# A hand-held order of instructions made anew: a decoder layer's queue table, planned with a longer hold of VectorE beside a POOL transfer issue

## The chip, the cores and the metric

The kernel runs on one core of one Trainium2 chip, in one launch. The metric is device microseconds of that core for the whole layer, lower is better. The engines are named as in the profile: PE is TensorE (PEld its weight loads), DVE is VectorE, ACT is ScalarE, POOL is GpSimd, SP is SyncE, which here only issues DMA transfers.

## The reference

One post-norm decoder layer, batch 1, sequence S = 512, width D = 1024, float32. Two token mixers read one combined projection; their gated sum is projected and added to the residual, and a gated FFN with a short convolution follows.

```python
h = x @ w_in[l]
y_a = nsa_attention(...) @ w_nsa_out[l]
y_b = gated_deltanet(...) @ w_gdn_out[l]
gate_a, gate_b = jnp.split(merge_gate, 2, axis=-1)
mix = (jax.nn.sigmoid(gate_a) * y_a + jax.nn.sigmoid(gate_b) * y_b) @ w_o[l]
x = layer_norm(DEEPNORM_ALPHA * x + mix, ln1_g[l], ln1_b[l])
f = conv_ffn(x, ffn_w_up[l], ffn_conv_w[l], ffn_w_down[l])
x = layer_norm(DEEPNORM_ALPHA * x + f, ln2_g[l], ln2_b[l])
```

The first mixer is sparse attention: 8 heads of 64 in two key groups, with three branches (compressed blocks, top-k selected blocks, a window), each a softmax with a linear position bias and a gate of its own. The second is gated DeltaNet: 4 heads of 128, a causal convolution of four taps and SiLU on q, k and v, and a chunked form with a triangular inverse per chunk of 64. The FFN is (silu(gate) * val) @ w_down, 2816 wide, after a causal convolution of three taps.

## The kernel before, in words

**Products.** Every large product is done with float32 split into a high and a low part. `split_w` (line 460) loads a block of weights into `raw` on SP's queue (line 463), rounds it into `wh` (line 470 on ACT, 472 on another engine) and takes the rest into `wl` (line 474, on DVE or POOL). `product` (line 479) then issues three matmuls for each contraction tile: wh with the high part (484), wh with the low part (486), wl with the high part (487). `raw`, `wh` and `wl` have three buffers each.

**Stages, by the time of the profile.** Until about 26 us x is transposed and split. From there to about 340 us steps of the two mixers are interleaved as a list ORDER says: for DeltaNet the projections with convolution (`conv_silu`, 635 to 655), `gdn_mid` (714 to 744), the triangular part `gdn_tri` (746 to 777) and `gdn_inv` (778 to 828); for the attention `cmp_attn` (993 to 1015: a softmax on DVE and ACT whose last step on DVE, line 1013, scales `cs`, which PE then transposes through `trans4`, line 659), `scores` (1030 to 1060) and `flip` (1062 to 1078). In `scores`, lines 1050 to 1059 take the reciprocal of a softmax's sum; where ACT scales the scores, DVE first multiplies the reciprocal by the gate (1056) and ACT scales (1057), and where POOL does, it does both in one operation (1059). From about 340 to 425 us come the merge gates (`merge`, 1118, a tanh at 1121) and the mixers' output projections (products into `pm`, merged at 1199 and 1201). The output projection with the first layer norm follows to about 490 us, then the FFN up to about 712 and the FFN down to the end.

**Sums in DRAM.** POOL issues transfers that add blocks of weights in DRAM (`sums_o`, line 503, into `osum`; `sums`, line 513, into `wsum`). `osum` is first read by a `raw` load on SP at 393 us, `wsum` after 700 us.

**What sets the order.** The instructions are emitted in one order by the program, with priorities. The table QUEUES (lines 133 to 333) then gives, for each of PE, DVE, ACT (as "Activation"), POOL and SP, the order in which that engine's instructions are to stand: each number is the n-th instruction of that engine in the program's order, a range stands for its members. The function `queues` (line 337) chains each engine's instructions in that order by scheduling-only dependencies. The instructions, tiles, buffers, engines and waits on data do not depend on the table; an engine works through its own list in order. The table comes from a planner outside the kernel that simulates the engines with a price for each operation.

Some numbers that the text below uses. PE: 452 is the first transpose of `cs` in `cmp_attn(0)` (line 659); 384-387 are four transposes of `kq` (line 659); 479 and 515-522 are matmuls of 128x512; 1969 is the last matmul of a `pm` product, 1942-1945 are matmuls of a `gps` product, and 1970 is the first matmul of the next `gps` product. POOL: 18 and 46 are `at` (line 743) of two heads, 31 is `th` (652), 32 `vraw` (653), 14 `rn` (525), 40 and 67 `wl` (474), 43 `grh` (720), 37 a cast of `vm` (1068), 29 and 30 tap sums (643), 64-66 `sc` (1059), 105 and 107 osum transfers (503), 140 and 141 wsum transfers (513). SP: 24 is the small load of `w` (line 939), 29-33 are `raw` loads.

Of the kernel before, what the change touches and what calls it, by code (L numbers as in the profile page):

```python
# [70 lines left out]
def layout(a):  # L71
# [72 lines left out]
488-489 752 740 490 509 491 741-742 492 541-542 753 493-494 754 743 495 510 496 543 511 546 755 497 544-545 512 547
756-757 498-499 744 758 500 548 759-760 549-551 560-561 761 745 762-765 562 565-566 766 552 767 746 553 768 554 537
555 591-592 563-564 567 538 568-569 539-540 581-582 769 570 593-596 556 597 557 598 558 599-600 770-771 559 571 583
585-586 796-797 772 584 572 798 573-575 773 587 601-602 576 799 577 774 800 588-589 801-806 603 606 590 604 651 578
605 607 579-580 807-810 608 653 811 620-621 609-611 652 812-813 654 814 612 815-816 622 625-626 613 623-624 614-616
864-865 627-628 641 629-630 642 866-870 617-618 871 619 643 645 872 631 646 873 644 632-633 874 634 875 647 876-877
635-636 699-700 648 637 649-650 638-639 878 640 701 879 704 702 880 817 705 881 703 818 882-886 706 718-719 707-709  # L150
887 720-721 819 838-839 722 710 655 659-660 656-658 661-662 840 854-855 711-712 841 663-666 842-843 713-715 856
667-669 671-678 670 857-858 716-717 844-845 679-686 860-861 859 846 862 687-694 863 1053 847-848 695-698 747-750
936-940 1054 941 1055 775 1056 776 1057 849 777-778 850 942-944 779 945-948 780 949-951 781-782 1058 952-954 783-784
# [24 lines left out]
1623-1624 1604-1605 1572 1625-1626 1573 1627 1574-1576 1628-1629 1634 1630-1632 1577-1579 1635-1638 1658 1639-1647
1580 1659 1648 1606-1609 1581 1660 1649 1661 1633 1650-1651 1662 1652 1663 1653 1664-1668 1654-1655 1669 1656
1670-1672 1657 1673 1682 1674-1676 1683 1677-1678 1684-1685 1679 1686-1687 1680 1688-1690 1694 1691 1681 1692-1693  # L180
1706-1707 1695-1696 1708 1697 1709-1711 1718 1712 1719 1713 1720 1698 1714 1699 1715 1721-1722 1700 1716 1701 1723
1717 1724-1725 1702 1726-1728 1703-1705 1729-1735 1754 1736-1737 1742-1746 1755 1747 1738 1748-1750 1739 1751 1756
1752 1757-1758 1753 1759-1772 1778-1779 1740-1741 1773 1780 1774 1781-1782 1775-1776 1783-1786 1777 1787-1789 1802
1790-1791 1803-1804 1814 1805-1807 1815 1808 1792 1809-1810 1816-1818 1811 1819-1820 1812 1821-1822 1813 1823-1825
1793-1794 1826 1795-1796 1827-1831 1797-1799 1832-1834 1800-1801 1835-1840 1850 1841-1842 1851-1855 1843 1856-1858
1844 1859-1861 1845 1862 1846-1849 1874-1878 1863 1879 1864 1886-1887 1865-1866 1880 1888 1867 1889 1881-1883 1868
1884 1869 1890 1885 1870 1891-1892 1898 1893-1897 1899 1871-1873 1900-1911 1922 1912 1923 1913-1914 1924 1915-1916
1925-1926 1917 1927-1928 1918 1929 1919 1930-1932 1920 1933-1934 1921 1935-1936 1946-1947 1937 1948 1938 1949 1958
1939-1942 1950-1954 1959-1960 1955-1956 1961 1957 1962-1964 1943-1944 1965-1969 1945 1970-1981 1994 1982 1995-1998
1983 1999 1984-1985 2000-2002 1986 2003-2004 1987 2005-2008 1988 2018 1989-1990 2019-2020 1991 2021 2009-2011 1992  # L190
2022-2024 2012-2013 2030 2014-2017 1993 2031 2025-2028 2032 2029 2033-2034 2042 2035 2043-2044 2036-2037 2054-2055
# [1380 lines left out]
```

## Time and profile before

| | before |
|---|---|
| median of 3 runs | 832.31 us (831.04 to 835.99) |
| the profiled execution | 831.55 us |
| its span, first to last instruction | 829.8 us |
| mean granted TensorE clock | 0.992 |
| PE busy | 809.2 us, 98% of the span |
| DVE, ACT, POOL busy | 602.5, 409.2, 180.5 us |
| moved by DMA | 119.58 MB, mean 144 GB/s |

The profile is one execution, the median is over others; the profiled execution's own time exceeds its span by what lies around the instructions. Times in rows are microseconds from the start of the span. A timeline row reads: start, duration, engine, source line, operation, output<-inputs, shapes, count, and in brackets the idle time of the engine before it with what ended the wait. A window row reads: window, its length, then busy time (count) of PE, PEld, DVE, ACT and POOL, the granted clock, the DMA engines' busy share, GB/s. A DMA row on an engine's own line is the issue of the transfer, not its flight.

### The profile page before, as it was taken

How to read it: one execution, taken by the hardware profiler on the slowest of the kernel's cores; microseconds unless marked ns; L12 is line 12 of the kernel's file. 1: busy time of each engine (PE TensorE's matmuls, PEld its weight loads, DVE VectorE, ACT ScalarE, POOL GpSimd, SP SyncE). 2: the span in 40 equal slices, each digit the busy share in tenths (PEclk: the TensorE clock that was granted, in tenths of full speed). 3: DMA queues.
4: the chain of work that ended last, by engine and by line, in shares of the span. 5: the costliest groups of instructions: out<-in, count | busy, mean ns of one | idle time of the engine just before them, and what ended most of it. 6: DMA issues, size and time to landing. Idle time of an engine off the chain costs nothing.

```text
span 829.8 us, 11767 instructions
## 1 busy us (share of the span) xinstructions
PE 809.2 (98%) x4138; PEld 673.8 (81%) x4138; DVE 602.5 (73%) x1339; ACT 409.2 (49%) x912; POOL 180.5 (22%) x176
## 2 busy tenths in 40 slices
PE   9999899999999999999999999999999999999996
PEld 8778688778888888888788898888888888878784
DVE  5656779979868976647549965667577577687897
ACT  4453487765576764513335333435334344574641
POOL 0333805141266111152200111102112101100001
PEclk9999999999999999999999999999999999999999
DMA  8333615134284711334365476333938932466583
GB/s 279 102 92 101 252 32 133 44 96 108 49 219 111 233 51 52 120 108 128 115 241 177 152 147 211 125 102 102 215 103 249 229 102 80 150 199 182 190 257 124
DMA packets 43979, 119.58 MB, mean 144 GB/s; under 512 B 3472, under 2 KB 4624, under 8 KB 43664
## 3 DMA queue, kind: packets, MB, share of 16 engines
q1 hardware_dynamic: 32144, 87.37, 32.3%
q0 software_dynamic: 11776, 31.46, 16.3%
q8 instruction: 33, 0.54, 0.3%
q14 instruction: 26, 0.21, 0.1%
HBM read 116.72 MB, written 33.55 MB: 181 GB/s over the span
## 4 chain that ended last, share of the span: by engine, by line
PE 82%; DVE 9%; DMA 4%; ACT 2%; issue 2%; POOL 1%; ACTq 0%; DVEq 0%; POOLq 0%; SPq 0%
PE pu L484 10%; PE pu L486 10%; PE pu L487 10%; PE gps L484 8%; PE gps L486 8%; PE gps L487 8%; DMA raw<-wsum 3%; PE pw L1288 3%; PE px L1452 3%; PE pu L1288 2%; PE pz L1452 2%; PE pout L1089 2%; PE pu L1452 2%; PE aps L1075 2%; PE pm L484 2%
## 5 line engine op out<-in xcount | busy, mean ns | idle before, releaser
L474 DVE TENSOR_TENSOR wl<-raw,wh 128x512 fp32r<-128x512 f32 x146 | 102.7, 705 | 78.0 <-ACT wh L470 38.6
L470 ACT ACTIVATE wh<-raw 128x512 fp32r<-128x512 f32 x126 | 79.1, 629 | 133.7 <-PE pu L486 97.0
L486 PE MATMUL pu<-ml,wh 128*128 128x512 f32 (+1 forms) x384 | 131.5, 373 | 0.0
L484 PE MATMUL pu<-mh,wh 128*128 128x512 f32 (+1 forms) x384 | 130.8, 372 | 0.4 <-ACT mh L1267 0.4
L487 PE MATMUL pu<-mh,wl 128*128 128x512 f32 (+1 forms) x384 | 130.8, 373 | 0.0
L484 PE MATMUL gps<-xh,wh 128*128 128x512 f32 x320 | 125.7, 404 | 3.2 <-ACT mt L1121 2.1
L486 PE MATMUL gps<-xl,wh 128*128 128x512 f32 x320 | 126.1, 401 | 0.0
L487 PE MATMUL gps<-xh,wl 128*128 128x512 f32 x320 | 124.4, 400 | 0.0
L484 PEld LDWEIGHTS pu<-mh,wh 128*128 128x128 f32 x384 | 71.3, 188 | 13.4 <-ACT mh L1267 0.7
L487 PEld LDWEIGHTS pu<-mh,wl 128*128 128x128 f32 x384 | 71.4, 188 | 13.0 <-DVE wl L474 0.5
L486 PEld LDWEIGHTS pu<-ml,wh 128*128 128x128 f32 x384 | 71.4, 188 | 12.6
L1410 DVE SCALAR_TENSOR_TENSOR fa<-pu,fcw,fa 128x511 f32<-128x511 f32 (+1 forms) x88 | 64.6, 744 | 17.5 <-ACT fa L1407 16.9
L1416 POOL TENSOR_TENSOR fth<-fth,fa 128x512 f32<-128x512 f32 x22 | 30.4, 1387 | 212.6 <-DVE fth L1415 186.3
L484 PEld LDWEIGHTS gps<-xh,wh 128*128 128x128 f32 x320 | 60.4, 190 | 15.1 <-issue 2.5
L487 PEld LDWEIGHTS gps<-xh,wl 128*128 128x128 f32 x320 | 60.8, 190 | 10.9
L486 PEld LDWEIGHTS gps<-xl,wh 128*128 128x128 f32 x320 | 61.0, 191 | 10.2
L1387 ACT ACTIVATE wh<-raw 128x512 fp32r<-128x512 f32 x67 | 40.1, 626 | 41.0 <-DMA raw<-in_down 13.5
L1388 DVE TENSOR_TENSOR wl<-raw,wh 128x512 fp32r<-128x512 f32 x67 | 44.8, 694 | 17.9 <-ACT wh L1387 17.3
L474 POOL TENSOR_TENSOR wl<-raw,wh 128x512 fp32r<-128x512 f32 x30 | 40.1, 1339 | 13.4 <-ACT wh L470 7.9
L525 POOL TENSOR_TENSOR rs<-rs,minus_half 128x1 f32<-128x1 f32 x8 | 7.2, 901 | 161.4 <-DVE rs L1246 161.4
L1407 ACT ACTIVATE fa<-pu,fcw 128x512 f32<-128x512 f32 x44 | 29.7, 680 | 24.8 <-PE pu L487 22.0
L1048 ACT ACTIVATE sc<-sc,mn 128x384 f32<-128x384 f32 (+2 forms) x64 | 35.7, 560 | 10.5 <-DVE mn L1046 10.1
(365 smaller groups left out, 1719.8 us busy)
## 6 DMA issues: line engine op xcount, KB each, us to landing
raw<-in_up SPq DMA_DIRECT2D x44, 512.0 KB, 3.7
raw<-in_wT SPq DMA_DIRECT2D x40, 512.0 KB, 3.6
wsum<-in_down POOLq DMA_DIRECT2D x6, 2816.0 KB, 20.8
raw<-wsum SPq DMA_DIRECT2D x20, 512.0 KB, 3.9
raw<-in_down SPq DMA_DIRECT2D x15, 512.0 KB, 4.3
osum<-in_wo POOLq DMA_DIRECT2D x6, 1024.0 KB, 9.0
wsum<-wsum POOLq DMA_DIRECT2D x2, 2816.0 KB, 14.6
raw<-in_wm SPq DMA_DIRECT2D x8, 512.0 KB, 3.5
```

What stands on the lines that cost most here:

```text
L470: A.activation(wh, r, AF.Copy)
L474: eng.tensor_tensor(wl, r, wh.bitcast(F32), op=OP.subtract)
L484: i = PE.matmul(ps, wh[k], mh_(k), start=(k == 0), stop=False)
L486: PE.matmul(ps, wh[k], ml_(k), start=False, stop=False)
L487: PE.matmul(ps, wl[k], mh_(k), start=False, stop=(k == n - 1))
L1048: A.activation(s[:, i, :n], s[:, i, :n], AF.Exp, scale=-1.0, bias=mn[:, 0, i:i + 1], accum_out=mn[:, 1, i:i + 1])
L1288: PE.matmul(ps[t], a[x](j)[:, ts], w[y][:, j % 2, :], start=fresh and j == 0 and i == 0, stop=j == TT - 1 and i == 2, skip_group_check=True)
L1387: A.activation(hi, raw[:, i], AF.Copy)
L1388: V.tensor_tensor(lo, raw[:, i], hi.bitcast(F32), op=OP.subtract)
L1410: V.scalar_tensor_tensor(acc[:, n:], ps[:, :S - n], w[:, i:i + 1], acc[:, n:], op0=OP.mult, op1=OP.add)
L1416: G.tensor_tensor(th, th, g[1], op=OP.mult)
L1452: m = PE.matmul(ps, a[x][:, j, ts], w[y], start=first and i == 0, stop=last and i == 2, skip_group_check=True)
```

## The change

Only the table QUEUES is replaced; no instruction, tile, buffer, engine or priority changes. The planner's prices had one rule added: a VectorE operation with two operands in SBUF that meets a transfer issue of POOL waits for POOL's next operation too. The table was made anew under it. 2349 of PE's 3880 places hold another instruction than before, 773 of DVE's 1275, 421 of ACT's 799, 91 of POOL's 172 and 15 of SP's 185. The first differences lie at 12 to 44 us; behind about 600 us no engine's order differs. Most instructions move by a few places. The core of the diff, with the lines that the text below speaks of:

```diff
     "PE": ...
-324-327 464-466 328 332-339 329-330 467 331 468-471 513 472 340-347 473 514 474-475 348-355 476-477 515 356-359 452
-384-387 516 478 517 479 501-502 453-455 412-415 518 503 519-521 504 522-526 440-441 527 442-443 723-724 528-529
...
+348-355 476-478 356-359 384-387 479 515-522 452 501 412-414 502 415 453-454 523-524 503 525-527 440-443 455 723-724
...
-1939-1942 1950-1954 1959-1960 1955-1956 1961 1957 1962-1964 1943-1944 1965-1969 1945 1970-1981 1994 1982 1995-1998
...
+1954 1961-1963 1955-1956 1964 1938 1965-1966 1939 1967-1968 1940 1957 1941 1969 1942-1945 1970-1991 1994-1997 1992
...
-    "Pool": """2 1 0 8 10 9 12 11 3 13 4-7 15-17 19-22 27-28 140 14 33 25 23 34 29 18 39 30 37 31 105 32 40 43 36 44 24 62 35 38 41
-45 54 107 48 26 55 104 42 49 51 47 52 92 66 108 68 67 46 65 64 69 57 50 58 109 87 56 53 59 61 63 75 60 144 77 80 110
...
+    "Pool": """2 1 0 8 10 9 11-12 3 13 4-7 15-17 19-22 27-28 33 23 25 34 141 140 29 39 30 18 31-32 14 40 37 43 105 24 38 26 44 36 35
+54 41 45 55 48 42 62 49 51 47 52 107 64 66 65 67 46 68 57 69 58 50 53 56 59 61 104 63 108 75 60 76 109 80 92 88 77 81
...
-    "SP": """0-7 17 8-9 15 25 10 12 11 13-14 19 18 16 20-23 26-28 24 29-75 80 76 79 77-78 81-134 136-165 167 135 169 171 173-178
...
+    "SP": """0-7 17 8-9 15 25 10 12 11 13-14 19 18 16 20-23 26-33 24 34-75 81 80 82-83 77-78 76 84 79 85-134 136-165 167 135 169
```

More of the change, by code (lines that the diff above doesn't have):

```diff
@@ L144 @@
[L144 to L153, printed above, removed]
@@ new lines @@
+1319-1320 1288-1289 1405-1406 1265-1266 1280 1267 1408 1268 1407 1281-1282 1269 1409 1270 1321-1323 1271 1324 1229
+1325 1290 1272 1326-1327 1291 1328-1329 1230 1330 1410 1292 1422 1293 1423 1294 1231 1411-1412 1232 1424 1413
+1425-1426 1295-1298 1414 1299-1301 1427 1302-1304 1379 1428 1415 1380-1381 1429 1416 1430-1432 1417-1419 1305 1382
+1443 1420 1444 1331-1332 1421 1383 1306 1384-1386 1433 1445 1447-1448 1387 1434 1388 1435 1389-1392 1436-1437 1333
+1449 1446 1393 1453 1477 1454 1478 1394 1438 1450 1455-1456 1451 1439 1395 1458 1452 1440 1396-1397 1479 1459 1480
@@ new lines @@
+1441 1481 1442 1482 1334 1460-1462 1457 1463 1472-1473 1398 1483-1485 1399-1401 1486 1402 1487-1488 1474 1464
+1501-1502 1465-1466 1475-1476 1467 1582 1489 1583 1490 1335 1503 1468 1517-1518 1339-1341 1504 1342 1336-1338
+1505-1506 1491-1494 1343-1346 1519-1520 1469 1495 1521 1470 1347-1348 1522 1351-1358 1349 1471 1507-1508 1350
+1509-1511 1496-1499 1512-1513 1359-1366 1523-1524 1544 1500 1545 1584-1585 1546 1367-1374 1525 1514 1547-1550
+1610-1611 1515-1516 1586-1588 1375-1378 1551 1526 1612-1613 1527 1552-1554 1589 1614 1528 1615 1563-1564 1529-1530
@@ new lines @@
+1590 1616 1591-1592 1531-1532 1617-1618 1533 1555 1619 1593 1534 1594 1535 1556 1595 1620 1596 1536-1537 1597-1598
+1538 1565 1599 1621-1622 1539-1540 1566-1567 1557-1558 1568-1569 1559 1600-1602 1541-1542 1570 1560 1571 1561
+1623-1626 1543 1562 1603 1627 1604-1605 1572-1577 1628-1629 1634 1630 1635 1631 1636-1639 1632 1640-1641 1578
+1606-1609 1579 1642-1643 1658 1644 1633 1645-1646 1580-1581 1647 1659-1660 1648 1661-1662 1649 1663-1667 1650-1651
+1668-1670 1652-1654 1671 1682 1655 1672 1656-1657 1673-1675 1683-1685 1676-1680 1686-1687 1681 1694 1688-1692 1695
@@ new lines @@
+1693 1706-1707 1696 1708-1709 1718 1697-1698 1710-1711 1699-1700 1712-1714 1701 1715-1716 1702 1719-1721 1703-1705
+1730 1722-1724 1717 1742 1725-1728 1731-1732 1743-1747 1733-1734 1754 1729 1755 1735 1748-1753 1736-1737 1756-1763
+1738-1740 1764-1769 1741 1770-1772 1778 1773-1774 1779 1775 1780-1782 1776 1783-1786 1777 1787-1788 1802 1789 1803
+1790 1804-1806 1814-1817 1807-1809 1818 1810-1811 1791 1812 1819 1792 1813 1793 1820-1822 1794 1823 1826 1795 1827
+1796 1824-1825 1828 1797-1798 1829-1830 1799-1800 1831 1801 1832-1838 1850-1852 1839-1840 1853-1858 1841 1859-1860
@@ new lines @@
+2035 2014 2036-2038 2015-2016 2042 2017 2029 2039 2043 2040 2054 2041 2055 2044-2051 2056 2052 2057-2059 2053
+2069-2070 2060 2071 2061 2066 2062-2063 2075-2076 2067-2068 2064-2065 2077 2072-2073 2081 2074 2090 2114 2093 2078
+2091 2094-2095 2099 2082 2092 2083 2096 2115 2079 2097 2117 2087 2098 2100-2101 2080 2084 2105 2118 2102 2106 2085
+2116 2103-2104 2108 2086 2088 2120-2121 2119 2089 2109 2123 2122 2107 2124-2126 2141 2129 2127 2142 2130 2110-2113
+2131 2135 2128 2132 2138 2143 2139 2133-2134 2136-2137 2140 2147-2149 2144-2145 2162 2146 2150 2163 2151-2156
@@ new lines @@
+2159-2160 2164 2161 2157-2158 2168-2170 2174-2176 2180-2182 2165-2167 2186-2187 2171-2173 2177-2178 2188 2179
+2189-2191 2195 2192-2193 2183-2185 2194 2196-2198 2210 2199-2200 2204-2206 2201 2211-2212 2202-2203 2207-2209
+2218-2220 2213 2224-2226 2221 2214 2230 2222 2215 2231-2232 2223 2236 2242 2227 2216 2243-2244 2228-2229 2245 2237
+2233-2235 2239 2274 2240 2238 2217 2250 2241 2338 2251-2252 2275 2306-2307 2276 2308 2253 2309 2254 2339 2310-2311
+2277-2278 2340 2255 2279 2246-2247 2256 2248 2280 2249 2341-2342 2312 2343 2313 2257 2281 2258 2282 2314 2344-2345
@@ new lines @@
+2259 2346-2347 2315 2283 2260 2284-2286 2348 2287 2316 2288 2261 2317-2319 2289-2290 2262 2291-2293 2263 2320-2321
+2264-2265 2349-2351 2266 2298 2294 2299-2300 2295 2322 2352-2353 2267 2301 2268-2269 2296 2354 2270 2302 2323 2303
+2355-2357 2271 2324 2304 2325 2297 2326 2358 2327 2330-2333 2359 2272 2328 2360 2273 2361 2329 2305 2362 2386 2410
+2434 2363 2387 2411 2364 2388-2390 2334-2337 2391-2392 2365 2393 2366 2435 2394-2395 2412 2396-2397 2436 2398 2413
+2367 2414 2399-2401 2437 2368 2415 2402 2416-2417 2438-2440 2418 2403-2407 2369-2374 2408-2409 2375 2419-2420
@@ new lines @@
+2441-2442 2376 2421 2443 2422 2377 2423 2444-2445 2378-2381 2424-2425 2382 2426 2383 2446 2384 2427-2428 2385 2429
+2482 2447-2449 2430 2483-2489 2450-2451 2431 2458 2490 2459-2460 2452 2432 2453 2433 2454 2461 2491-2492 2455
+2462-2463 2493 2464 2494-2495 2465-2472 2496 2456-2457 2497-2499 2506-2512 2473 2513 2474 2514-2516 2500-2501 2517
+2475 2502 2476-2478 2518-2519 2503 2479-2481 2520-2524 2504-2505 2530-2535 2525-2527 2536-2545 2528 2554 2546 2529
+2547 2555 2548-2551 2556 2552 2557-2558 2553 2559-2568 2578 2569-2570 2579-2589 2571-2572 2590-2591 2602 2592 2573
@@ new lines @@
+2593 2603-2605 2574-2576 2606-2610 2594 2577 2611 2595 2612-2613 2596-2599 2626-2627 2614 2628 2615 2629-2631 2600
+2632 2616 2601 2617 2633-2636 2618-2621 2637-2638 2650 2622 2639 2623 2640-2642 2651 2643 2624-2625 2652-2653 2644
+2654-2656 2645-2646 2657-2661 2647 2662 2648 2663-2666 2674 2667 2675 2649 2668 2676 2669-2671 2677-2678 2672-2673
+2679-2684 2698-2699 2685 2700-2706 2686 2707-2709 2687 2710 2688-2690 2722 2711 2723-2724 2691-2692 2725-2726
+2712-2714 2727-2728 2693-2695 2729 2715 2696 2716 2730 2717 2697 2731-2734 2718 2735 2719 2736 2720 2746-2748
@@ new lines @@
+2737-2739 2749-2751 2740 2752-2753 2741 2754-2755 2721 2756 2742 2757-2758 2743 2759 2770-2771 2760-2761 2772 2762
+2773 2744 2774-2776 2763 2777 2745 2778-2780 2764-2766 2781 2767 2794 2782 2795 2768-2769 2783 2796-2799 2784-2788
+2800-2802 2789-2792 2803-2804 2793 2805-2806 2818 2807-2808 2819-2820 2809 2821 2810-2815 2822-2824 2816 2825 2817
+2826-2830 2842-2843 2831 2844 2832-2833 2845-2849 2834 2850-2852 2835 2853 2836 2854-2860 2866 2837 2867 2861 2868
+2838 2869 2862 2870 2839-2840 2871-2874 2863 2875 2864 2841 2876-2878 2865 2879-2881 2890-2891 2882 2892 2883
@@ new lines @@
+2893-2902 2884-2886 2903 2914-2915 2904 2916-2917 2887 2918-2920 2905 2921 2888 2906 2922-2925 2889 2907-2908 2926
+2909 2927 2910 2938 2928 2939-2941 2911 2942-2943 2912-2913 2944 2929 2945-2950 2930-2931 2951 2962 2932 2963 2952
+2964-2965 2953-2954 2933 2966 2955 2967-2968 2934 2969 2935 2970-2971 2936 2972 2956 2973 2957-2959 2937 2960 2986
+2974-2975 2987 2961 2976-2978 2988-2991 2979 2992-2993 2980 2994 2981 2995-2996 2982 2997-3002 2983 3003 3010
+2984-2985 3004 3011-3012 3005 3013 3006-3007 3014 3008 3015 3009 3016-3018 3034 3019-3022 3035-3042 3023 3043-3044
@@ new lines @@
+3024 3045 3025-3026 3046 3027 3058 3047 3028-3029 3059 3048 3060 3030 3049 3061 3050 3031 3062-3063 3051 3032-3033
+3052 3064 3053 3065-3069 3054 3070-3071 3055 3082 3056-3057 3083-3091 3072 3092-3093 3073-3076 3106 3077-3078
+3094-3095 3107 3096 3108 3079 3109 3080-3081 3110-3113 3097-3098 3114-3116 3099-3100 3117 3101 3118 3102 3130-3131
+3103-3104 3132-3133 3105 3134-3137 3119 3138-3140 3120 3141-3142 3121 3143 3122-3125 3154 3126 3155-3156 3144 3157
+3145 3127-3129 3158 3146 3159-3162 3147 3163-3169 3178 3170 3179 3171 3180 3148 3181 3172 3182-3186 3149-3152 3173
@@ new lines @@
+3153 3187-3188 3174 3189-3190 3175 3191 3176 3192 3177 3202 3193-3194 3203-3206 3195-3200 3207-3214 3201 3226
+3215-3218 3227 3219-3220 3228 3221 3229 3222 3230 3223-3225 3231-3236 3250 3237 3251-3252 3238-3239 3253-3254 3240
+3255-3261 3241 3262-3263 3242-3244 3264 3274 3245 3275-3276 3265 3246-3247 3277-3280 3248 3281 3266 3249 3267
+3282-3286 3268-3269 3287 3270 3298 3271 3288-3289 3299 3272 3300 3290-3291 3301 3292 3302-3303 3273 3304-3306
+3293-3294 3307 3295 3308 3296 3309-3312 3322 3297 3313-3314 3323 3315 3324-3330 3316-3317 3331-3332 3318 3333-3335
@@ new lines @@
+3319 3336 3320 3346 3337-3338 3347 3339-3342 3348-3349 3343-3344 3350-3352 3345 3353 3370 3354 3321 3355 3371
+3356-3361 3372 3362 3373-3379 3363 3380 3364-3365 3381 3366-3367 3394-3395 3382 3368 3396 3383 3397-3402 3384 3403
+3369 3404 3385-3387 3405 3388-3390 3406 3391 3407 3392 3408 3418-3419 3409 3420 3393 3421-3424 3427 3410 3428 3411
+3429 3425 3412 3426 3413 3430-3431 3433-3434 3414 3435 3432 3436-3437 3439 3438 3440-3441 3415-3416 3442 3445-3446
+3443-3444 3447 3451 3448 3417 3449 3452-3453 3450 3454-3464 3466 3487 3465 3467 3469-3471 3475 3468 3488 3484-3485
@@ new lines @@
+3617 3549 3618 3599-3600 3604 3609 3605 3622 3621 3625 3606 3623-3624 3610 3626-3628 3611 3631 3629 3632 3630 3633
+3637 3613 3634-3635 3638-3639 3636 3640 3643 3641 3612 3642 3646 3614 3647 3644-3645 3615 3649 3648 3652-3653
+3650-3651 3654 3658 3655-3657 3661 3659 3662-3663 3660 3664 3685 3667 3665 3668 3666 3686 3682 3669 3673 3670 3687
+3691 3683 3671 3674 3672 3675 3679 3684 3692 3676 3688 3680 3689 3681 3690 3693-3694 3677 3695 3697 3696 3700
+3698-3699 3678 3701 3703 3702 3706 3704 3707 3705 3708-3714 3718-3719 3715-3716 3720 3717 3724 3721 3725-3726
@@ new lines @@
+3722-3723 3730 3727 3731 3728 3732 3729 3751 3733-3734 3752 3735 3739-3740 3736 3741 3745 3748-3749 3737 3750 3754
+3738 3742 3753 3746 3755 3747 3757 3743 3758 3756 3759-3760 3744 3761 3763 3762 3764 3766 3765 3769-3771 3767-3768
+3772 3775 3773-3774 3778-3779 3776-3777 3780 3784 3781-3783 3785 3787 3786 3790-3792 3796-3798 3788-3789 3802-3803
+3793 3804-3806 3794 3807 3795 3799-3801 3808-3820 3847-3848 3821-3825 3849 3826 3850-3851 3827-3828 3852-3853 3829
+3854-3855 3830-3836 3856 3837 3857 3838-3842 3858 3843-3844 3859 3845-3846 3860-3879""",
+    "DVE": """0 27 104 1-4 6 5 7 9 8 10-11 13 12 14-18 58-60 19 64 61 20 65 23 21-22 90 66 62 31-32 67 63 33 72 34-38 73 39 102
@@ new lines @@
+1008 990 999 1011 991 1012 1020 982 1002 993 1003 1021 1009 1024 968 1010 994-995 971 1025 1031 1004 1032 1013 1022
+1014 992 1035 1023 981 1036 1015 1044 1017 1045 1026-1027 1018 1048 1033-1034 1019 1037 1049 1055 1038 1056 1028 1016
+1059 1046-1047 1039 1006 1005 1060 1068 1050 1057 1069 1051 1072 1052 1058 1073 1041 1079 1061 1053 1062 1042 1080
+1040 1083 1054 1043 1070-1071 1074 1084 1075 1063 1092 1029-1030 1093 1096 1085 1065-1066 1086 1081 1097 1082
+1103-1104 1107 1076 1087 1094-1095 1108 1089 1078 1116 1088 1090 1098 1117 1099 1105 1064 1077 1120 1100 1091 1106
@@ L334 @@
+147 138-139 142 150 143 145 153 148 146 149 151-152 154-155 157 156 160 159 158 161 163 162 165 164 166-171""",
+    "SP": """0-7 17 8-9 15 25 10 12 11 13-14 19 18 16 20-23 26-33 24 34-75 81 80 82-83 77-78 76 84 79 85-134 136-165 167 135 169
+171 173-178 168 179-180 172 182 166 170 181 183-184""",
 }
```

286 lines of the change are left out of this document (102 added, 184 removed).

## The prediction

> **What bounds the kernel now.** I read the page's totals first.
>
> ```profile
> span 829.8 us, 11767 instructions
> PE 809.2 (98%) x4138; PEld 673.8 (81%) x4138; DVE 602.5 (73%) x1339; ACT 409.2 (49%) x912; POOL 180.5 (22%) x176
> PE 82%; DVE 9%; DMA 4%; ACT 2%; issue 2%; POOL 1%; ACTq 0%; DVEq 0%; POOLq 0%; SPq 0%
> ```
>
> TensorE is busy for 98% of the span and holds 82% of the chain that ended last. The diff adds and removes no instruction, so a new order can only win the time in which PE stands still or runs at half clock. The windows by stage tell where that is. Their columns are window, length, busy time of PE, PEld, DVE, ACT and POOL with counts, granted clock, DMA share, GB/s.
>
> ```profile
> 80.00:180.00 100.00, 93.74 (x592) 77.46 (x593) 83.73 (x266) 67.93 (x200) 43.93 (x47) 0.97 0.38 117
> 180.00:340.00 160.00, 159.77 (x963) 135.69 (x963) 122.99 (x386) 102.74 (x285) 47.73 (x47) 1.00 0.44 112
> 340.00:420.00 80.00, 77.67 (x335) 63.49 (x334) 46.89 (x71) 21.56 (x41) 22.49 (x22) 0.98 0.38 119
> 600.00:822.00 222.00, 221.12 (x963) 179.54 (x961) 168.13 (x271) 106.40 (x177) 22.23 (x17) 1.00 0.56 167
> ```
>
> PE is idle for 6.26 us between 80 and 180 and 2.33 between 340 and 420. Of these only those two show a granted clock under 1.00. Behind 600 us PE hardly stops (0.88 of 222), and no place in the tables moves there: that part has nothing to give or to lose. Looking closer at the weak stages finds three stalls, each followed by a stretch at half clock.
>
> ```profile
> 99.72:102.69 2.97, 0.00 (x1) 0.01 (x1) 2.97 (x2) 0.38 (x1) 2.91 (x4) 1.00 0.99 360
> 102.94:106.36 3.42, 3.42 (x14) 3.03 (x13) 0.75 (x4) 1.48 (x6) 0.97 (x1) 0.50 0.30 115
> 168.20:169.35 1.15, 0.00 (x1) 0.01 (x1) 1.15 (x5) 0.46 (x2) 0.50 (x1) 1.00 1.03 417
> 171.21:174.62 3.41, 3.41 (x27) 2.33 (x25) 1.80 (x5) 1.41 (x5) 2.08 (x3) 0.50 0.16 28
> 404.03:406.09 2.06, 0.00 (x1) 0.03 (x1) 1.19 (x2) 0.74 (x2) 2.06 (x2) 1.00 0.00 0
> 406.73:410.14 3.41, 3.41 (x10) 2.62 (x9) 3.01 (x7) 1.79 (x4) 0.00 (x0) 0.50 0.48 157
> ```
>
> Call them A (2.97 us), B (1.15) and C (2.06). A stretch of 3.41 us at 0.50 does 1.70 us less work than one at 1.00, so the three cost 6.18 + 5.10 = 11.3 us at most. That is the purse.
>
> **The change part by part: stall A.** In the timeline rows (start, duration) the stall is made by VectorE and POOL together.
>
> ```profile
> 98.12 4.52 DVE L1013 TENSOR_TENSOR cs<-cs,csm 128x512 f32<-128x512 f32 x1
> 96.56 1.28 POOL L652 TENSOR_TENSOR th<-th,acc 128x512 f32<-128x512 f32 x1 [0.46 <-ACT th L648]
> 97.78 0.76 POOL L503 DMA_DIRECT2D osum<-in_wo  x1
> 98.50 1.35 POOL L653 TENSOR_TENSOR vraw<-th,acc 128x512 f32<-128x512 f32 x1
> 99.74 1.33 POOL L474 TENSOR_TENSOR wl<-raw,wh 128x512 fp32r<-128x512 f32 x1
> 100.96 1.11 POOL L720 TENSOR_TENSOR grh<-cst,gdh 128x512 fp32r<-128x512 f32 x1
> 102.69 0.33 PE L659 MATMUL aps<-ident,cs 128*128 128x128 f32 x1 [2.97 <-DVE tiny L578]
> L1013 DVE TENSOR_TENSOR cs<-cs,csm x2: 684/2600/4516, 98.1 to 216.3; 128x512 f32<-128x512 f32 x2
> ```
>
> L1013 takes 0.684 us the other time and 4.516 here. It starts inside the osum issue and ends only when grh does, after three POOL operations that read SBUF back to back. PE's transpose at L659 (452 in the table) needs its result. The rule behind the new table has this shape, but it prices the hold at the issue and one operation, to 99.85, where the row shows three.
>
> The new table does two things. PE's run "384-387 479 515-522" now stands before 452: four transposes and nine large matmuls. Their prices:
>
> ```profile
> 457.85 3.40 PE pw L1288 x15
> 199.15 0.77 PE dps L659 x7
> ```
>
> The first gives 0.227 us each, the second 0.11, so the cover is 9 x 0.227 + 4 x 0.11 = 2.5 us and PE comes to 452 at 99.72 + 2.5 = 102.2. On POOL the transfer (105) goes from before vraw (32) to behind grh (43), and at (18) and rn (14) come into the run: "18 31-32 14 40". If that run has a gap, L1013 ends near 98.12 + 0.68 and the stall is gone. If not, from th's start it lasts at, th, vraw, rn, wl = 1.28 + 1.28 + 1.35 + 1.28 + 1.33 (at and rn estimated as th), to 103.1; L1013 ends at 103.8 and the gap is 1.6. I take the middle, 0.8, since nothing shows which: 2.17 less. The half clock goes in one case and stays in the other, 0.85 on average. **A: -3.0, bounds -1.4 (gap 1.6, slow stretch stays) and -4.7.**
>
> [...]
>
> ```profile
> 139.38 0.68 DVE L655 SCALAR_TENSOR_TENSOR kq<-th,acc 128x512 f32<-128x512 f32 x1
> 139.35 0.75 POOL L503 DMA_DIRECT2D osum<-in_wo  x1
> ```
>
> A two-input operation of 0.68 us that lies wholly in an issue of 0.75 is not stretched. So the issue is not enough; the unbroken run behind it counts.
>
> **Stall B** is the same hold without an issue beside it.
>
> ```profile
> 166.25 2.54 DVE L1056 TENSOR_TENSOR mn<-mn,gsig 128x1 f32<-128x1 f32 x2
> 166.19 1.29 POOL L474 TENSOR_TENSOR wl<-raw,wh 128x512 fp32r<-128x512 f32 x1
> 167.42 1.28 POOL L743 TENSOR_TENSOR at<-at,cst 128x512 f32<-128x512 f32 x1
> 170.95 0.56 POOL L1059 TENSOR_SCALAR sc<-sc,mn,gsig 128x256 f32<-128x256 f32 x1 [2.25 <-DVE mn L1050]
> 169.35 0.33 PE L1075 MATMUL aps<-ident,sc 128*128 128x128 f32 x1 [1.15 <-ACT sc L1057]
> ```
>
> Two products of one column take 2.54 us, over wl and at. In the new table these (67 and 46) stand behind sc (64-66), which waits for a reciprocal after 168; so POOL waits while mn runs. A hold of over 2 us leaves, more than the 1.15 that PE lost; the gap goes. Of the 1.70 of half clock I count half, as smaller gaps just ahead stay (1.32 us at 164.18, quoted below) and 1.15 was enough for a slow stretch. What is behind sc now, wl first, comes up to 3 us later, and its product waits for it; PE has other products there. **B: -2.0, bounds -1.15 and -2.85.**
>
> **Stall C** is a chain through the merge.
>
> ```profile
> 403.84 0.69 DVE L1199 SCALAR_TENSOR_TENSOR mt<-mt,pm 128x512 f32<-128x512 f32 x1 [1.58 <-PE pm L487]
> 405.35 0.60 ACT L1121 ACTIVATE mt<-gps 128x512 f32<-128x512 f32 x1 [8.61 <-DVE mt L1201]
> 406.09 0.47 PE L484 MATMUL gps<-xh,wh 128*128 128x512 f32 x1 [2.06 <-ACT mt L1121]
> ```
>
> PE's 1969 ends pm, then L1199, L1201 and the tanh follow, and 1970 needs the buffer that the tanh frees. Before, one matmul (1945) stood between; now four (1942-1945). Three more at 0.227 are 0.68: the gap falls to 1.38. B's 1.15 called up a slow stretch, so I leave this one in. **C: -0.7, bounds -0.7 and -2.4** (slow stretch gone too).
>
> **The other moved places** number 2,300 on PE and 770 on VectorE. They cost nothing where PE has other products ready, which the 159.77 of 160 us show for the old order. The old order also left a gap of 1.32 where DVE was late:
>
> ```profile
> 164.18 0.33 PE L659 MATMUL dps<-ident,z 128*128 128x128 f32 x1 [1.32 <-DVE z L775]
> 393.20 0.39 SPq L1171 DMA_DIRECT2D raw<-osum  x1
> 66.51 2.89 SPq L463 DMA_DIRECT2D raw<-in_wT  x2
> 76.57 0.32 PE L977 MATMUL aps<-cu,w 64*128 64x62 f32 x1
> raw<-in_wT SPq DMA_DIRECT2D x40, 512.0 KB, 3.6
> ```
>
> Newly made places can misfit likewise. I charge one such gap and half a slow stretch, 1.32 + 0.85. **+2.2, bounds 0 and 4.7 (another A: 2.97 + 1.70).**
>
> The osum and wsum transfers mostly go later, by up to some 50 us, to about 320 us at the latest (two more move inside the FFN's up projection, whose sums are read in the down projection). The first reader of an osum on SP is at 393.20, so at least 70 us cover them; without cover a landing would hold PE for its length. On SP the small load of w (24) passes behind five raw loads, the last of them issued near 69.4 (66.51 + 2.89). PE reads it at 76.57, so 7 us are left for a load and its landing, where one of 512 KB lands 3.6 us after its issue. Covered, with 3.5 us to spare; if a raw load ahead slips by more, PE waits for the difference. The raw loads come no later. I count nothing for these.
>
> **Sum:** -3.0 - 2.0 - 0.7 + 2.2 = -3.5 on the profiled execution's 831.55 (span 829.8 and 1.75 around it) = 828.05. The median of the runs shown stands 0.76 above that execution: **828.8**. Its own bounds: all best, -4.7 - 2.85 - 2.4 = -9.95, is 822.4; all worst, -1.4 - 1.15 - 0.7 + 4.7 = +1.45, is 833.8.
>
> [...]
>
> **The rivals.**
>
> *The issue isn't the cause.* VectorE is held by any unbroken POOL run, so moving issues only moves the meeting: A stays at 2.97 with its slow stretch. B and C give 1.15 + 0.68, the misfits take 2.2, so +0.35: median 832.7. For it: kq at 139.38, and B without an issue. Against: PE's longer cover before 452 helps whatever holds L1013. This is also the case in which the change doesn't do what it says.
>
> *All three go and nothing comes back:* 822.4, the best bound. For it: 159.77 of 160 us show that an order without gaps can be had. Against: so many places moved.
>
> *The two issues 141 and 140 hold L1005 (slower).* Before, wsum's issue stood alone; now both stand together, ahead of the run "29 39 30 18 31-32 14 40".
>
> ```profile
> 80.63 1.23 POOL L513 DMA_DIRECT2D wsum<-in_down  x1
> 93.49 0.97 DVE L1005 TENSOR_TENSOR cs<-cs,cmx 128x512 f32<-128x512 f32 x1
> ```
>
> L1005 heads the softmax whose end is L1013. A hold here of the size of L1013's (4.52 - 0.68 = 3.84) plus one more issue (1.23) and one more operation (1.28) is 6.35 late. If L1013 is then held as before, 452 waits 2.97 + 6.35 - 2.5 = 6.8 us: 3.85 more than A, and a second slow stretch, 1.70. With B, C and misfits (-2.0 - 0.7 + 2.2): +5.05, median 837.4. It decides once POOL starts two-input operations without a gap for over 4 us while L1005 is ready. Against: before, L1005 met the same kind of run and lost only 0.3, and a wait for ACT's taps breaks it.
>
> **How the numbers follow.** Forecast 0.48, issue not the cause 0.22, all gone 0.16, L1005 held 0.14. A measurement of this kernel can tell about 1%, 8.3 us: 824.0 and 840.6 are the borders. Faster: 0.13 from "all gone" and 0.03 from the forecast's lower edge, 0.16. Slower: 0.06 from L1005 with another misfit and 0.04 elsewhere, 0.10. Same: 0.74. The range, 822 to 838, leaves out about one in ten on each side.
>
> **What would show it.** Right: L1013's first instance under 1.5 us or its gap under 1.6; mn near 0.3 us with sc ahead of wl; the gap before PE's 1970 near 1.4; a clock under 1.00 in at most two windows. Wrong: L1013 or L1005 over 3 us behind the paired issues; a gap over 2 us on PE at a place not named here; any difference behind 600 us.

## The result, and the profile after

The changed kernel takes **838.13 us** (median of 7 runs, 835.56 to 840.94), the one before 832.71 (7 runs, 831.04 to 835.99): a ratio of 1.0058, 95% interval 1.0031 to 1.0085. It is slower by 0.6% (the interval leaves 1 out), where 828.8, a gain, was forecast and 822 to 838 given: 0.13 us above the upper edge, and in the other direction. The profiled execution took 838.13 us, with a span of 836.3 (6.5 above before) and a mean granted clock of 0.987.

The shares of the chain that ended last, by engine, and the windows by stage of the changed kernel, with the columns as before:

```profile
PE 78%; DVE 9%; DMA 5%; issue 3%; ACT 2%; POOL 1%; SPq 0%; ACTq 0%; DVEq 0%
```

```profile
80.00:180.00 100.00, 97.87 (x641) 82.25 (x640) 81.91 (x279) 74.07 (x225) 44.94 (x45) 1.00 0.39 122
180.00:340.00 160.00, 146.16 (x868) 122.69 (x867) 117.29 (x359) 88.43 (x246) 45.66 (x47) 0.95 0.42 103
340.00:420.00 80.00, 78.54 (x347) 64.67 (x346) 50.65 (x79) 27.15 (x49) 21.82 (x22) 1.00 0.41 128
```

PE's share of the chain fell from 82 to 78%, and "issue" rose from 2 to 3. Both weak stages of before got better: from 80 to 180 PE is idle for 2.13 us instead of 6.26, at a clock of 1.00, and from 340 to 420 for 1.46 instead of 2.33. The loss stands in the stage that had been almost without a gap: 13.84 us idle of 160, clock 0.95. The windows of that stage show where.

```profile
214.26:216.14 1.88, 0.00 (x1) 0.03 (x1) 1.85 (x3) 0.63 (x2) 0.84 (x1) 1.00 0.87 342
216.20:219.80 3.60, 3.60 (x15) 2.92 (x16) 2.92 (x10) 0.88 (x4) 1.23 (x1) 0.69 0.19 19
245.91:256.92 11.01, 0.00 (x1) 0.00 (x0) 2.02 (x2) 0.75 (x3) 5.24 (x7) 0.61 1.11 240
257.00:261.00 4.00, 4.00 (x15) 3.51 (x16) 3.96 (x8) 3.32 (x16) 1.09 (x1) 0.50 0.56 173
```

PE stands for 11.01 us in one piece, and goes on at half clock (0.50 from 257 to 261). The chain of waits through that piece (start, duration, what):

```profile
237.79 1.29 POOL acc L638
239.08 12.60 issue
251.67 0.68 POOL osum L498
252.36 1.28 POOL th L647
...
253.82 1.06 POOL so L520
...
254.90 1.25 DVE so L884
...
256.17 0.70 ACT y L662 x2
...
256.92 1.33 PE dps L654 x5
```

(Lines below the table are five lower than before.) POOL is done with `acc` at 239.08 and next has a transfer to issue, the copy of osum2 into osum3 (110). It starts it at 251.67. "issue" says that the profile shows nothing it waited for. Behind it in POOL's order stands the operation of line 520 for DeltaNet's output norm, then VectorE, ScalarE, and PE's transpose of `y`. The transfer rows of the stretch from 225 to 245 give what was under way (KB each, us to landing):

```profile
wsum<-in_down POOLq DMA_DIRECT2D x1, 2816.0 KB, 20.5
osum<-in_wo POOLq DMA_DIRECT2D x1, 1024.0 KB, 21.9
```

and the timeline of POOL gives their issues:

```profile
230.89 1.76 POOL L508 DMA_DIRECT2D wsum<-in_down  x1
...
234.61 1.17 POOL L498 DMA_DIRECT2D osum<-in_wo  x1
...
251.67 0.68 POOL L498 DMA_DIRECT2D osum<-osum  x1 [12.60 <-issue]
```

230.89 + 20.5 = 251.4: POOL stood until the wsum0 addition had landed (its copy starts at 251.67). The copy reads nothing that this addition writes. In the kernel before, the same copy went out without standing while the same addition was under way (it landed at 243.53):

```profile
222.48 1.79 POOL L513 DMA_DIRECT2D wsum<-in_down  x1
...
233.46 0.69 POOL L503 DMA_DIRECT2D osum<-osum  x1
```

There the osum0 addition (106) came only at 261. The new table had moved it up between the two.

Where the 6.5 us of span come from is told by the start of the same place of PE's order in the two traces, that is, of the n-th instruction, whichever it is (before, after, difference; us):

```
place  420    93.2    91.8    -1.41
place  480   106.5   101.0    -5.47   stall A
place  780   165.8   159.7    -6.16
place  840   176.7   167.4    -9.31   stall B
place 1020   214.7   206.5    -8.17
place 1080   226.5   221.5    -5.01   the gap at 214
place 1200   248.1   243.8    -4.32
place 1260   258.9   268.3    +9.47   the gap at 246
place 1920   392.5   401.3    +8.81
place 1980   409.9   416.7    +6.74   stall C
place 3840   811.6   818.4    +6.78
```

The new order is 9.3 us ahead after 176 us, gives 1.1 and 3.2 back at two places, loses 13.8 at another, and wins 2.1 at C.

### The profile page after: what moved, and what is told of

It reads as the page before. It is cut to its first block, busy times and chain, and to the rows that moved or that the text cites. A ratio compares the mean times of both kernels' runs of the same rounds, so it can differ in the third digit from the quotient of the medians.

```text
span 836.3 us, 11778 instructions
## 1 busy us (share of the span) xinstructions
PE 807.5 (97%) x4138; PEld 672.4 (80%) x4138; DVE 600.8 (72%) x1339; ACT 408.4 (49%) x912; POOL 181.0 (22%) x176
## 4 chain that ended last, share of the span: by engine, by line
PE 78%; DVE 9%; DMA 5%; issue 3%; ACT 2%; POOL 1%; SPq 0%; ACTq 0%; DVEq 0%
PE pu L479 9%; PE pu L481 9%; PE pu L482 9%; PE gps L479 8%; PE gps L481 8%; PE gps L482 8%; PE pout L1084 2%; DMA raw<-in_down 2%; DMA raw<-wsum 2%; DVE wl L1383 2%; PE pm L481 2%; PE pm L479 2%; PE pz L1447 2%; PE pm L482 2%; PE aps L1070 2%
## 5 line engine op out<-in xcount | busy, mean ns | idle before, releaser
L469 DVE TENSOR_TENSOR wl<-raw,wh 128x512 fp32r<-128x512 f32 x146 | 104.9, 723 | 75.3 <-ACT wh L465 33.8
L1383 DVE TENSOR_TENSOR wl<-raw,wh 128x512 fp32r<-128x512 f32 x67 | 44.8, 693 | 19.2 <-ACT wh L1382 18.7
```

Source lines behind the costliest of these rows:

```text
L469: eng.tensor_tensor(wl, r, wh.bitcast(F32), op=OP.subtract)
L1383: V.tensor_tensor(lo, raw[:, i], hi.bitcast(F32), op=OP.subtract)
```

## Experiments

Theory when they were planned, an inference from the one stand of 12.60 us: POOL's transfer queue has room for so much under way; two adding transfers (2816 and 1024 KB) fill it, and POOL stands at the third issue. Rival: the copy waits for the wsum0 addition as such. No trace shows the queue itself, so the runs can tell only when POOL stands and until when.

**1. The osum0 addition moved back.** The changed kernel with one place of POOL moved:

```diff
-87 144 90 78 106 84 71 110 72 86 70 73 93 85 74 94 82 91 95 89 96-99 79 100 ...
+87 144 90 78 84 71 110 72 86 70 73 93 85 74 94 82 91 95 89 96-99 106 79 100 ...
```

> The changed kernel with one place moved: the osum0 addition (106 on POOL) goes from behind wl 78 to behind wl 99, so that only the wsum0 addition (144) is under way when POOL comes to the osum3 copy (110). Theory: POOL stood 12.6 us at 110 because two adding transfers, 2816 and 1024 KB, were still under way in its queue and a third found no room; with one ahead there is room, as before at 233.46. Then 110 starts within 1 us of the operation ahead of it, PE's 11.01 us gap and the half clock behind it go, and the time is 838.1 - 13.8 (the lag that PE gained between its places 1200 and 1260) = 824.3, 822.5 to 827. Rival: 110 waits for the wsum0 addition itself, whatever else is under way; then POOL still stands there until some 20 us after 144, and the time is 836 to 840.

Measured 824.81 us (6 runs), ratio to before 0.990 (0.9879 to 0.9922). POOL's row of the copy, and the stage, in this kernel:

```profile
237.66 0.72 POOL L498 DMA_DIRECT2D osum<-osum  x1
```

```profile
180.00:340.00 160.00, 157.14 (x934) 132.05 (x934) 126.71 (x377) 97.65 (x262) 45.99 (x47) 1.00 0.44 112
```

The copy goes out as soon as `acc` is done, with the wsum0 addition still under way (229.53, landing 20.6 later). The whole loss of the change, and more, hung on one place of one transfer.

**2. The same move made in the kernel before.**

```diff
-... 63 75 60 144 77 80 110 90 76 ... 94 82 106 91 95 ...
+... 63 75 60 144 106 77 80 110 90 76 ... 94 82 91 95 ...
```

> The kernel before with one place moved: the osum0 addition (106 on POOL) from 261 us to right behind the wsum0 addition (144, 222.48), ahead of the osum3 copy (110, 233.46). Theory of room in POOL's transfer queue: 110 now stands until the wsum0 addition has landed, near 243.5 to 245, so POOL idles 9 to 11 us, and PE loses 3 to 13 us behind sc and wl: 836 to 846. Rival, that 106 has no part in it: 110 starts near 234.7 as before, and the time is 831.5 to 834.5.

Measured 842.81 us (4 runs), ratio 1.0113 (1.009 to 1.0135). POOL's timeline:

```profile
222.03 1.78 POOL L513 DMA_DIRECT2D wsum<-in_down  x1
222.99 2.06 POOL L503 DMA_DIRECT2D osum<-in_wo  x1
...
242.49 0.68 POOL L503 DMA_DIRECT2D osum<-osum  x1 [9.45 <-issue]
```

In its other surroundings the same pair brings the same stand, again to the landing of the wsum0 addition (222.03 + 20.1 = 242.1; the copy starts at 242.49). It costs 10 us.

**3 and 4. What makes POOL stand.** The changed kernel, its order untouched; once the osum0 addition is halved, so that half of that sum is left out, once it is made a copy, so that one addend is left out. Both kernels compute something else and serve for this question alone.

```diff
+            if (to, add) == (0, 1):
+                G.dma_start(out=osum[to][:, :TT // 2], in_=src[:, :TT // 2], accum_op=OP.add)
+                continue
```

> The changed kernel, its order as it is, with the osum0 addition (106) cut to half its rows; the other half of that sum is left out. If the room is counted in rows or bytes, half of 106 may let 110 in at once: no POOL gap over 1 us at 110, 823 to 827. If two transfers (or two adding ones) under way are the limit whatever their size, 110 stands until the wsum0 addition has landed, about 251, with a POOL gap of 11 to 13 us: 836 to 840.

```diff
-        todo = [(0, o[0, :, 0], 0), (1, o[0, :, 1], 0), (0, o[0, :, 1], 1), (1, o[1, :, 1], 1), (2, osum[1], 0), ...
+        todo = [(0, o[0, :, 0], 0), (1, o[0, :, 1], 0), (0, o[0, :, 1], 0), (1, o[1, :, 1], 1), (2, osum[1], 0), ...
```

> The changed kernel, its order as it is, with the osum0 addition (106) made a plain copy of the same 1024 KB, so that one addend of that sum is left out. If an adding transfer takes more room than a copy of the same size, or only adding ones count, 110 finds room: no POOL gap over 1 us, 823 to 827. If two transfers under way of any kind are the limit, or bytes alone count, POOL stands 11 to 13 us at 110: 836 to 840.

One run each: 826.22 us with half the addition, 825.78 with a copy. The osum3 copy in the one and in the other:

```profile
240.36 0.71 POOL L501 DMA_DIRECT2D osum<-osum  x1
```

```profile
239.49 0.65 POOL L498 DMA_DIRECT2D osum<-osum  x1
```

Neither stands, with as many transfers under way as in the changed kernel (in the second one they were issued at 231.35 and 235.08 and landed 20.9 and 21.3 us later, so both were under way at 239.49): their number alone does not make POOL stand. With the copy the KB are the same as there too (2816 + 1024 ahead, 1024 to issue), so the KB alone do not either. The kernel before shows this in a run that leaves nothing out. Two additions of 1024 KB (issued at 261.24 and 267.49, landed at 270.29 and 278.93) were under way when a copy of 2816 KB was issued; that is the same 4864 KB, and POOL did not stand:

```profile
267.49 1.11 POOL L503 DMA_DIRECT2D osum<-in_wo  x1
268.17 1.55 POOL L513 DMA_DIRECT2D wsum<-in_down  x1
```

So the same KB made POOL stand for 12.60 us with two additions of 2816 and 1024 KB ahead, and not at all with a copy for the second one. How much more an addition counts than a copy is not shown. An estimate from these five places: in the changed kernel a copy of 1024 KB went in 272 packets (212 to 217 us) and an addition of 1024 KB in 528 (217 to 227). If each 2 KB row of a copy counts once and of an addition twice, the two stands came at 2816 + 1024 + 512 = 4352 (twice 1408 rows, twice 512, once 512), and the three issues without one at 3840 (experiments 3 and 4) and 3456 (before, 268.17); that additions alone count would fit as well.

**5 and 6. Does the issue make stall A?** The forecast held that the unbroken run of POOL operations matters, and the issue not. The kernel before, with transfer 105 behind `grh`, and with it one place further back only:

```diff
-... 37 31 105 32 40 43 36 ...
+... 37 31-32 40 43 105 36 ...      (5)
+... 37 31-32 105 40 43 36 ...      (6)
```

> The kernel before with the transfer issue 105 moved on POOL from ahead of vraw (98.5) to behind grh, all else in place: stall A without an issue beside L1013. Rule behind the table (the issue and one operation hold): no issue is met, L1013 takes 0.7 us, its stall of 2.97 us on PE and the half clock go, 827 to 829. Theory of the unbroken run: L1012 or L1013 is held from 97.9 until grh has ended, near 101.4, and gets in at the issue; the PE gap stays at 1.8 to 2.6 us, with or without a slow stretch, 830 to 833.

> The kernel before with the issue 105 moved by one place, to between vraw and wl: L1013's chain meets the issue in the middle of the run. Theory of the unbroken run: an issue reads no SBUF operand, so it is a break; L1012 and L1013 get in while it runs, near 99.2 to 100.1, PE's gap before 452 shrinks from 2.97 to under 0.6 us and the half clock goes, 827 to 830. Rule behind the table: the meeting with the issue holds through wl, to 101.3 or later; gap 1.9 to 2.7 us, 830 to 833.

Measured 829.04 us (10 runs), ratio 0.9952 (0.9932 to 0.9972), and 829.34 (8 runs), 0.9955 (0.9935 to 0.9976). The rows of the fifth:

```profile
97.88 1.32 POOL L653 TENSOR_TENSOR vraw<-th,acc 128x512 f32<-128x512 f32 x1
99.16 1.72 POOL L474 TENSOR_TENSOR wl<-raw,wh 128x512 fp32r<-128x512 f32 x1
```

```profile
98.08 1.67 DVE L1013 TENSOR_TENSOR cs<-cs,csm 128x512 f32<-128x512 f32 x1
```

and of the sixth:

```profile
98.93 0.76 POOL L503 DMA_DIRECT2D osum<-in_wo  x1
```

```profile
97.87 1.66 DVE L1013 TENSOR_TENSOR cs<-cs,csm 128x512 f32<-128x512 f32 x1
```

With no issue beside it, in the very same run, L1013 lasts past the end of the one operation that is under way (vraw, to 99.20) and ends at 99.75; now POOL's next wl gives way to it (1.72 us against 1.33 before). The theory of the unbroken run is dead: it had 1.8 to 2.6 us of gap for the fifth, and the gap is under 0.2 (PE's last matmul ends at 99.68, the transpose starts at 99.80). The table's rule expected 0.7 us for L1013 and at most 829; it took 1.67, and the time lies just above. In the sixth an issue that comes at 98.93, while L1013 already waits (from 97.87), does not hold it (1.66 us): there the table's rule expected a gap of 1.9 to 2.7 us and had none, and it is the other theory's time (827 to 830) that came.

**7 and 8. The hold that the new table made itself.** In the kernel of experiment 1, VectorE's `wl` at 212.28 lost 2.9 us just behind the issue of the osum2 copy (108), as in the changed kernel, whose rows these are:

```profile
212.06 3.60 DVE L469 TENSOR_TENSOR wl<-raw,wh 128x512 fp32r<-128x512 f32 x1
```

```profile
211.38 0.65 POOL L498 DMA_DIRECT2D osum<-osum  x1
212.01 0.63 POOL L467 CAST wh<-raw 128x512 fp32r<-128x512 f32 x1
212.58 1.30 POOL L738 TENSOR_TENSOR at<-at,cst 128x512 f32<-128x512 f32 x1
213.82 1.28 POOL L469 TENSOR_TENSOR wl<-raw,wh 128x512 fp32r<-128x512 f32 x1
```

```diff
-... 104 63 108 75 60 76 109 ...
+... 104 63 75 108 60 76 109 ...      (7, and 8)
-... 1968 1940 1957 1941 1969 1942-1945 1970 ...
+... 1968 1957 1969 1940-1945 1970 ...      (PE, 8 alone)
```

> The kernel of the first experiment (osum0 addition moved back, 824.8) with the osum2 copy (108) moved by one place, to behind the cast 75 and ahead of at 60. There VectorE's wl (212.28) took 3.58 us over at and wl of POOL, with no issue in progress, and PE stood 1.87 us. Now the wl meets the issue. Theory: the issue is a break, wl takes 0.7 us, PE's gap is under 0.3 us: 822.0 to 824.0. Rule behind the table: wl waits for the issue and for at, 2.4 us or more; the gap is 0.7 to 1.9 us: 823.7 to 825.5.

> The kernel of the experiment with 108 moved, and on PE two more gps matmuls (1940, 1941) moved from ahead of 1969 to behind it, so that six stand between the end of pm and 1970. Stall C, 1.47 us in the kernel of the first experiment, shrinks by 2 x 0.23 to 1.0 us; 0.5 us less than the run beside it, 821.5 to 823.5, too small for the timing and to be seen in the gap alone. If the gap before 1970 stays at 1.4 to 1.5, the merge chain does not start from pm's last matmul.

Measured 821.84 us (6 runs), ratio 0.987 (0.9844 to 0.9896), and 823.20 (6 runs), 0.9879 (0.9851 to 0.9906). Their profiles disagree about the same place (first the seventh, then the eighth; POOL's issue, then VectorE's wl):

```profile
212.06 0.65 POOL L498 DMA_DIRECT2D osum<-osum  x1
...
212.15 0.69 DVE L469 TENSOR_TENSOR wl<-raw,wh 128x512 fp32r<-128x512 f32 x1
```

```profile
212.02 0.65 POOL L498 DMA_DIRECT2D osum<-osum  x1
...
212.11 3.62 DVE L469 TENSOR_TENSOR wl<-raw,wh 128x512 fp32r<-128x512 f32 x1
```

Both times `wl` starts 0.09 us into the issue; once it goes, once it loses two turns (a turn is an operation of POOL that it waits for). So a meeting is not always paid for, and this pair tells nothing for either side. The longer cover at the merge did not shrink stall C (1.44 us against 1.47 in the seventh). The two L1194 run one behind the other from the end of the first `pm`, not of the last; here they started 0.23 us earlier against PE's last matmul before the gap, and L1196 behind them then took 0.89 us instead of 0.69.

**9. The issue taken away from there**, ten microseconds ahead:

```diff
-... 104 63 108 75 60 76 109 ...
+... 104 108 63 75 60 76 109 ...
```

> The kernel of the first experiment (824.8) with the osum2 copy (108) moved on POOL by one place ahead, before z 63, so that it is issued near 200, some 10 us ahead of the cast 75, at 60, wl 76. VectorE's wl then starts near 212 as before, beside the cast and just ahead of at, but no issue is near. If the issue is what makes VectorE lose its turn (the table's rule, and the run with 105 behind grh), wl takes 0.7 us, PE's gap of 1.87 us goes, 821.5 to 823.8. If a cast followed by two back-to-back operations is enough, wl takes 3.5 us again, the gap stays, 824 to 826.

Measured 821.96 us (4 runs), ratio 0.987 (0.9839 to 0.9901). The time is that of the first theory, but neither duration of `wl` came:

```profile
212.28 1.74 DVE L469 TENSOR_TENSOR wl<-raw,wh 128x512 fp32r<-128x512 f32 x1
```

```profile
212.22 1.26 POOL L738 TENSOR_TENSOR at<-at,cst 128x512 f32<-128x512 f32 x1
213.44 1.72 POOL L469 TENSOR_TENSOR wl<-raw,wh 128x512 fp32r<-128x512 f32 x1
```

`wl` met `at`, waited for it alone (1.74 us, to 214.02; `at` ends at 213.48), and POOL's wl gave way (1.72 us against 1.27 in experiment 1). PE's gap of 1.87 us is gone (it is idle for 0.17 us between 212 and 218). The cast ended at 212.25, just before `wl` started, so the rival of a cast is not quite put to the test here. Stall B before is the comparison: there too VectorE started 0.06 us into an operation of POOL behind a cast, but 0.63 us after an issue, and it lost two turns instead of one. This is the best version that does not rest on a lucky meeting: 1.3% under the kernel before, 1.9% under the changed one by the medians (821.96 against 838.13).

**10. Stall B once more.** The forecast called it a hold without an issue. But one had ended 0.63 us ahead of `mn` (164.93 + 0.69 = 165.62, mn at 166.25):

```profile
164.93 0.69 POOL L503 DMA_DIRECT2D osum<-osum  x1
```

The kernel before, with that issue moved behind sc:

```diff
-... 92 66 108 68 67 46 65 64 69 ...
+... 92 66 68 67 46 65 64 108 69 ...
```

> The kernel before with the osum2 copy (108) moved on POOL from 164.93, ahead of the cast 68, wl 67 and at 46, to behind sc 64, after 170: stall B without an issue in the 0.7 us ahead of mn. Theory: only an issue in progress or just ended makes VectorE lose more than one turn; the two products mn, which took 2.54 us over wl and at, now take 1.4 us or less, PE's gap of 1.15 us falls below 0.3 and the half clock behind it goes: 829 to 831. Rival, the unbroken run: mn is held over wl and at again, 2.5 us, gap 1.1, 832 to 834.

Measured 830.27 us (10 runs), ratio 0.9969 (0.9957 to 0.9982). The two products, and PE's windows there and behind:

```profile
166.83 0.62 DVE L1056 TENSOR_TENSOR mn<-mn,gsig 128x1 f32<-128x1 f32 x2
```

```profile
165.00:171.00 6.00, 6.00 (x60) 5.18 (x58) 5.33 (x18) 4.98 (x16) 5.00 (x7) 1.00 0.00 0
171.00:177.00 6.00, 6.00 (x60) 4.91 (x61) 4.22 (x10) 4.35 (x18) 2.68 (x3) 1.00 0.81 258
```

0.62 us instead of 2.54, beside the same wl and at (`mn` now comes 0.74 us into wl, before 0.06); no gap, no half clock there.

## Why the prediction was wrong, point by point

**The step that failed** is the sentence on the transfers: "so at least 70 us cover them; without cover a landing would hold PE for its length ... I count nothing for these." It asked who reads a sum and when. It did not ask what POOL does at an issue when earlier transfers are still under way, and so priced the moves of 106 (261 to 235) and 144 (222 to 231) at nothing; 106 in fact moved earlier, where the text said "mostly go later". It cost 13.8 us (places 1200 to 1260): 11.01 of standing and the half clock behind. Experiments 1 and 2 show it from both sides, with the rest of the order unchanged. No bound of the sum covered it: the worst for new misfits was 4.7. Without that one place the changed kernel is at 824.81, inside the range and on the forecast side; its gain is 7.75 us (against 832.56), where the terms were summed to 3.5. That 838.13 lies so near the range's edge, and near the 837.4 of the rival on L1005, is luck: the range had no such loss in it, and that rival did not happen.

**Stall A**, forecast -3.0, came to -4.1 (places 420 to 480), within its bounds. L1013 is not held, and PE has cover:

```profile
98.97 1.08 POOL L520 TENSOR_TENSOR rn<-ss,minus_half 128x4 f32<-128x4 f32 x1
```

```profile
99.42 0.68 DVE L1008 TENSOR_TENSOR cs<-cs,csm 128x512 f32<-128x512 f32 x1
```

The reason given beside the sum, that "the issue is not enough; the unbroken run behind it counts", was wrong. Experiment 5 leaves the run and takes the issue: 4.52 us become 1.67.

**Stall B**, forecast -2.0, -3.2 from place 780 to 840; all 30 products mn now take 143 to 160 ns. That it was "the same hold without an issue beside it" was wrong too (experiment 10).

```profile
L1051 DVE TENSOR_TENSOR mn<-mn,gsig x30: 143/153/160, 109.0 to 326.0; 128x1 f32<-128x1 f32 x30
```

**Stall C**, forecast -0.7, came to -2.1. The gap went from 2.06 to 1.46, as forecast (1.38), but no half clock followed (1.00 from 414.4 to 420). Leaving that stretch in was the mis-sized term, by about 1.4 us (2.1 against 0.7). That it stayed away may be chance: a gap of 1.88 us was followed by a slow stretch at 217 in this kernel, and one of 1.87 us at the same place in experiment 1 by none.

**New misfits**, forecast +2.2: one such place, the wl at 212.06, cost 3.2 with its gap of 1.88 and part of a slow stretch. Another 1.1 went between places 840 and 1020, where PE has a gap of 0.66 at 191.62. So this term was mis-sized too, and but for the stand at 246 within its bounds.

**The rivals.** "The issue isn't the cause" (0.22) fell with experiments 5, 9 and 10; the rule behind the table points the right way, though not every meeting is paid for (experiments 6 and 7) and a paid one cost two or three turns, not one. "All three go and nothing comes back", 822.4, did not come either: C kept 1.46 us and the wl at 212.06 was new. "The two issues 141 and 140 hold L1005" did not happen; the operation lies inside the second issue unstretched:

```profile
88.19 2.31 POOL L508 DMA_DIRECT2D wsum<-in_down  x2
```

```profile
89.65 0.68 DVE L1000 TENSOR_TENSOR cs<-cs,cmx 128x512 f32<-128x512 f32 x1
```

The small load of `w` on SP had its cover: no gap of PE shows at it.

So the change did what it says. Its rule took the holds of A and B away. The same planning, which as it seems has no price for a stand of POOL at an issue, put a second addition in front of a copy and lost more than it had won.

## What to carry to other kernels

Before a transfer is moved on an engine that issues transfers and computes, list what is under way in that queue at its new place, with sizes and landing times: here POOL stood for 12.60 us at an issue behind two additions, everything behind it in its order stood too, and the profile called that wait only "issue". A planner that has no price for a wait will sooner or later run into it, so look at the changed kernel's longest idle "issue" of each engine first. And when one place costs as much as here, undo that place alone before judging the rest of an order: this table was 1% better than the old one, less one number.

## What the runs showed of the hardware

**POOL at an issue behind two additions.** 2816 KB and 1024 KB of additions ahead made POOL stand at a copy of 1024 KB for 12.60 us (changed kernel) and 9.45 us (experiment 2), until the first had landed; half of the second (experiment 3), or a copy in its place (experiment 4), let it through at once (one run each).

**VectorE beside an issue.** In the traces of the two kernels, every two-operand VectorE operation that took over 2 us (4.52 and 2.54 before, 3.60 in the changed one) began during an issue or at most 0.63 us after one, and lasted over two or three operations of POOL; so did the wl near 212 in experiments 1, 3, 4 and 8 (3.58, 3.60, 3.55 and 3.62 us). Far from an issue, such an operation lost one turn at most in these two traces, 1.1 us (L1201 before: 1.78 us instead of 0.69 at 371.52, 101.8 us after an issue), and in experiments 5 and 9 POOL's next operation then gave way (1.72 us, against 1.33 and 1.27). Why an issue costs further turns, and why it did not in experiment 7 (0.69 us), stays open. One operation of one operand was long as well: a cast of VectorE at 256.06 in the changed kernel took 2.31 us (another of its shape 0.41 at 103.95), over two operations of POOL and 3.7 us after an issue.

**The half clock.** A gap of 1.88 us was followed by a clock of 0.69 over 3.6 us in the changed kernel, and one of 1.87 us at the same place in experiment 1 by none:

```profile
216.40:219.90 3.50, 3.50 (x19) 2.67 (x19) 3.05 (x11) 0.88 (x4) 1.23 (x1) 1.00 0.23 16
```

The length of a gap did not tell in these traces whether a slow stretch came: 1.15 us at 168.20 before was followed by one (0.50 from 171.21), 1.32 at 162.85 before and 1.46 at 412.84 in the changed kernel by none (1.00 from 164.5 to 171.2 and from 414.4 to 420). So half clocks are to be forecast here as chances.
